# A third seven-product pair in gate and up, and the decay masks of the state-space mixer on ScalarE, in a two-layer hybrid decoder trunk

## The chip, the cores and the metric

The kernel runs on one core of a Trainium2 chip. A core has five engines with an instruction stream each: TensorE (PE, matrix products; its weight loads are listed as PEld), VectorE (DVE), ScalarE (ACT), GpSimd (POOL) and SyncE (SP, which here issues the large DMAs). The metric is the time of one execution on the device in microseconds (us); of several runs the median is given.

## The reference

The input is one sequence of 256 positions and 2048 features in float32. Each of the two layers does:

```
h    = rms_norm(x)
proj = h @ w_in                          # 2048 x 6608 (6672 in the second layer)
y    = concat(retention(proj), mamba2(proj), rwkv7(proj))
x    = x + y @ w_out                     # 2048 x 2048
h    = rms_norm(x)
x    = x + (silu(h @ w_gate) * (h @ w_up)) @ w_down    # d_ff = 5632
```

and a last rms_norm follows. Inside the state-space mixer (mamba2, 16 heads in two groups of 8, chunks of 128 positions) the part that matters here is

```
a        = dt * A                                       # decay logs, per position and head
seg      = a_cum[i] - a_cum[j]
decay_in = exp(where(i >= j, seg, -inf))                # 128 x 128 per head and chunk
y_diag   = ((C B^T) * decay_in) @ x
```

## The kernel before, in words

**Products in three terms.** Every float32 weight tile is split into a high part (`wh`, a cast to the type fp32r that TensorE multiplies) and a low part (`wl`, the difference), the activations likewise (`xh`, `xl`), and a product is the sum of three matmuls: high by high, high by low, low by high.

**The weights' way.** The kernel knows the whole list of its weight tiles in advance (`plan`). `fetch` (L291) issues a DMA of 512 KB per tile on SP's queue into one of 5 buffers `raw`; `split` (L300) makes the halves, with the cast on ScalarE (L307) and the subtraction on VectorE (L308), into 3 buffers each of `wh` and `wl`. `wtile` is called where TensorE's next tile is needed: it splits up to two parts further than that one and keeps fetching ahead of the splits.

**Stages of a layer.** The input projection has 14 groups of columns (`dense`, L366, matmuls L382 to L392), 8 tiles of 256 rows each, taken in the order of a list. While they run, three lanes of generators work through the mixers: `ret` (retention), `ssm` (state space) and one for rwkv. After each half tile `pump` (L162) advances the lanes in turn until one engine's estimated load since then reaches its credit (VectorE 0.35, ScalarE 0.9, POOL 0.8, TensorE 0.8, in us by a simple estimate per instruction). A generator that yields a number waits that many turns. A scheduler then fixes the order of the instructions on each engine; each engine works strictly in that order.

The output projection has 4 groups of 8 tiles; behind each group `post_pair` (L424) transposes the new activations and splits them for the FFN. The FFN runs in a part of 6 and one of 5 blocks of 512 columns; each block is one call of `gate_up` (L1288), 22 in both layers, and each part is followed by its down projection.

**Gate and up.** A call makes four results C: two halves of the rows by gate and up. Its 2048-long sum is cut into 8 pairs `kp` of 128-row tiles. An ordinary pair is eight block products of 128x128 by 128x512, 24 matmuls, in two parts `c` of 12. A pair in the tuple `SEVEN` is treated as a 2x2 block matrix product and takes seven products, by a scheme of the Strassen and Winograd kind, 21 matmuls in three parts: s0 (9), s1 (6) and s2 (6). Four of the seven products collect over the pairs of `SEVEN` in accumulators of their own (`mx` in the profile) and are added into the results once, after the last pair of `SEVEN`, by the additions on VectorE behind L1325. All of these matmuls are recorded as L1294.

For such a pair `split` makes sums of the weight blocks first: `u1` (L329, 1024 wide, from the two tiles of the pair, so both must have landed), the two halves of `u2` (L331, L332, 512 wide each), then three halvings L307/L308 (of the tile itself, of `u1` and of `u2`) and one half-width halving of the fourth block (L335 on ScalarE, L336 on VectorE). An ordinary pair has two halvings. The sums of the activations are made once per layer in `post_pair`: four 128x128 subtractions and additions on POOL (L106), a 512-wide cast on ScalarE and a 512-wide subtraction on VectorE. On the host, `_pairs` lays out the four blocks of such a pair accordingly.

**The masks.** `ssm_dt` (L995) makes the decay logs: for each of four blocks (chunk by group) `masked(i)` multiplies a triangular 128x128 matrix of ones by the decay log of each of 8 heads, for the high part `ah` and the low part `al` of the log. The result, 128x1024 for each part, is multiplied by another triangular matrix on TensorE (L1080, L1081), which sums it to the wanted differences, and ScalarE takes the exponential. The products are one POOL instruction per 128x1024 result (L106, `u<-cc,ah` and `u<-cc,s`), 8 per layer. Also on POOL, and in the same part of the layer, are the inverse square roots of the rwkv lane (L106, with `negh`) and a part of retention's rotary products (L106, `u<-u,cc` 128x256).

Of the kernel before, what the change touches and what calls it, by code (L numbers as in the profile page):

```python
# [9 lines left out]
AF = mybir.ActivationFunctionType  # L10
ALU = mybir.AluOpType
PSUM = bass.MemoryType.PSUM

P = 128
# [9 lines left out]

FFN_PARTS = [6, 5]

SEVEN = (2, 5)

# [27 lines left out]
class Trunk:  # L58
# [194 lines left out]
    def plan(self):  # L253
# [7 lines left out]
        for l in range(DEPTH):  # L261
# [7 lines left out]
            for nf in FFN_PARTS:  # L269
                for f in range(f0, f0 + nf):  # L270
                    for kp in range(8):
                        t = [("wgu", ((l * 11 + f) * 16 + 2 * kp + j) * P * 1024, 512) for j in range(2)]
                        if kp in SEVEN:
                            parts += [(f"s{j}", len(seq)) for j in range(3)]
# [149 lines left out]
    def post_pair(self, kp, src, scale, xh, xl):  # L424
# [10 lines left out]
        self.tt(fl(xl), w[:, :512], fl(xh).bitcast(F32), ALU.subtract)  # L435
        if kp in SEVEN:
            a11, a21, a12, a22, s1, s2, s3, q = [w[:, i * P:(i + 1) * P] for i in range(8)]
# [557 lines left out]
    def ssm_dt(self, l, raw):  # L995
# [17 lines left out]
        p = self.S(33)[:, :32]  # L1013
# [26 lines left out]
        for t in range(2):  # L1040
            o = self.U()
# [9 lines left out]
            self.mm(ps, M["Bt"][:, g * P:(g + 1) * P], xe[:, g * 512:(g + 1) * 512])  # L1051
            self.act(st[:, g * 512:(g + 1) * 512], ps, AF.Copy)
        yield
        tl = self.cst("tril").rearrange("p (o c) -> p o c", o=1).to_broadcast([P, 8, P])

        def masked(i):
            r = []
            for ap in (ah.bitcast(F32), al):
                m = self.U(F32R)
                self.tt(m[:, :1024].rearrange("p (h c) -> p h c", h=8), tl,  # L1060
                        ap[:, 8 * i:8 * i + 8].rearrange("p (h o) -> p h o", o=1).to_broadcast([P, 8, P]),
                        ALU.mult, eng="pool")
                r.append(m)
                yield 2
            return r
        ahead = yield from masked(0)
        y = M["y"] = [None, None]
        dsk = self.par(l, "dsk")
        for t in range(2):
# [3 lines left out]
            for g in range(2):  # L1073
                ma = ahead
                if t + g < 2:
                    ahead = yield from masked(2 * t + g + 1)
# [12 lines left out]
                for j in range(8):  # L1089
                    h = 8 * g + j  # L1090
# [197 lines left out]
    def gate_up(self, rstd):  # L1288
# [9 lines left out]
        for kp in range(8):  # L1298
            xk = [self.xs(2 * kp + j) for j in range(2)]
            A = lambda t, k: tuple(h[:, t * P:(t + 1) * P] for h in xk[k])  # L1300
            if kp not in SEVEN:
                for k in range(2):
# [4 lines left out]
            else:  # L1307
                cb = self.comb[kp]
                S1, S2, S3, Q = [(cb[:, i * P:(i + 1) * P], cb[:, 512 + i * P:512 + (i + 1) * P]) for i in range(4)]
                first, last = kp == SEVEN[0], kp == SEVEN[-1]  # L1310
                if first:
# [11 lines left out]
            if kp == 0:  # L1323
                self.flush()
            if kp == SEVEN[-1]:  # L1325
                t0, t1, sg = self.U(), self.U(), self.U()
# [164 lines left out]
def _pairs(a, b):  # L1491
# [4 lines left out]
    for kp in range(k):  # L1496
        if kp in SEVEN:
            o[kp, 0, :, 0], o[kp, 0, :, 1], o[kp, 1, :, 0], o[kp, 1, :, 1] = \
# [93 lines left out]
```

## Time and profile before

| | |
|---|---|
| median of 3 runs | 2423.09 us (2422.21 to 2423.18) |
| profiled execution | 2423.65 us, of which the span of the instructions is 2421.6 us |
| granted TensorE clock, mean over the span | 0.996 |
| PE busy | 2389.3 us (99% of the span) |
| DVE busy | 1675.4 us (69%) |
| ACT busy | 1206.7 us (50%) |
| POOL busy | 152.1 us (6%) |
| HBM read | 430.66 MB, 179 GB/s over the span |

A row of a timeline gives the start, the duration, the engine, the line, the operation with its output and inputs, and in brackets the engine's idle time before it with the instruction that ended it. A row of the groups gives the count, the busy time and the mean in ns of one instruction, then the idle time before them and its releasers. A row of the windows gives busy time and count for each engine, then the granted clock as a share of the full one, the share of the DMA engines and GB/s. Matmuls are pipelined: their durations overlap, and what one costs is the distance between two starts.

### The profile page before, as it was taken

The page shows a single profiled execution, that of the slowest core. Times are in us where ns is not written, and L with a number is a line of the kernel's source. Part 1 is how long each engine was busy: PE and PEld are TensorE (multiplying, and loading weights), DVE is VectorE, ACT ScalarE, POOL GpSimd, SP SyncE. Part 2 cuts the span into 40 slices and gives each one's busy share as a digit, 9 for nine tenths or more (in the row PEclk, how much of TensorE's full clock was granted, in tenths as well). Part 3 has the DMA queues.
Part 4 walks back from the last instruction along what each step waited for, and adds up shares of the span by engine and source line. Part 5 has one row for each costly group of instructions (what it writes and reads, how often), then busy time and mean ns, then how long its engine had stood idle before and what let it go on. Part 6 is the DMA issues. An engine that isn't in the chain of part 4 may idle for free. (4 is left out here: it accounts for less than half of the span.)

```text
span 2421.6 us, 33651 instructions
## 1 busy us (share of the span) xinstructions
PE 2389.3 (99%) x13076; PEld 2023.5 (84%) x13076; DVE 1675.4 (69%) x2106; ACT 1206.7 (50%) x1506; POOL 152.1 (6%) x157
## 2 busy tenths in 40 slices
PE   8999899999999999999999999999999999999998
PEld 8998788888888878888899988887888888888886
DVE  7777756577886467876558876565878754688754
ACT  6445545555554345554454546455555543455543
POOL 2100320000000000000001113200000000000000
PEclk9999999999999999999999999999999999999999
DMA  8454345556555555565544544445555655555654
GB/s 290 147 170 115 133 154 174 179 184 202 192 197 190 189 188 194 187 213 191 184 164 143 165 122 153 157 165 182 192 195 188 200 191 191 184 197 196 215 187 144
DMA packets 139424, 436.01 MB, mean 180 GB/s; under 512 B 30464, under 2 KB 30720, under 8 KB 139264
## 3 DMA queue, kind: packets, MB, share of 16 engines
q1 hardware_dynamic: 137360, 428.52, 53.4%
q0 software_dynamic: 1184, 4.19, 0.5%
q8 instruction: 102, 1.67, 0.3%
q10 hardware_dynamic: 720, 1.15, 0.1%
q14 instruction: 58, 0.48, 0.1%
HBM read 430.66 MB, written 3.15 MB: 179 GB/s over the span
## 5 line engine op out<-in xcount | busy, mean ns | idle before, releaser
L308 DVE TENSOR_TENSOR wl<-raw,wh 128x1024 fp32r<-128x1024 f32 (+3 forms) x763 | 928.0, 1218 | 494.2 <-ACT wh L307 487.2
L307 ACT ACTIVATE wh<-raw 128x1024 fp32r<-128x1024 f32 (+3 forms) x763 | 793.8, 1042 | 893.1 <-PE dn L391 443.4
L1294 PE MATMUL dn<-wh,xh 128*128 128x512 f32 x1100 | 431.4, 392 | 2.3 <-DVE res L103 2.3
L1294 PE MATMUL dn<-wl,xh 128*128 128x512 f32 x1100 | 428.6, 390 | 0.0
L1294 PE MATMUL dn<-wh,xl 128*128 128x512 f32 x1100 | 428.5, 390 | 0.0
L391 PE MATMUL dn<-wh,u 128*128 128x512 f32 x920 | 363.4, 395 | 0.0
L390 PE MATMUL dn<-wh,u 128*128 128x512 f32 x920 | 363.0, 395 | 0.0
L392 PE MATMUL dn<-wl,u 128*128 128x512 f32 x920 | 362.1, 394 | 0.3 <-DVE wl L308 0.2
L382 PE MATMUL dn<-xh,wh 128*128 128x256 f32 x896 | 258.8, 289 | 7.8 <-ACT wh L307 7.8
L384 PE MATMUL dn<-xh,wl 128*128 128x256 f32 x896 | 254.8, 286 | 1.1 <-DVE wl L308 1.1
L383 PE MATMUL dn<-xl,wh 128*128 128x256 f32 x896 | 255.1, 285 | 0.0
L1294 PEld LDWEIGHTS dn<-wh,xh 128*128 128x128 f32 x1100 | 206.5, 188 | 48.9 <-DVE u L103 3.9
L1294 PEld LDWEIGHTS dn<-wl,xh 128*128 128x128 f32 x1100 | 206.4, 188 | 43.4
L1294 PEld LDWEIGHTS dn<-wh,xl 128*128 128x128 f32 x1100 | 206.6, 188 | 42.1
L390 PEld LDWEIGHTS dn<-wh,u 128*128 128x128 f32 x920 | 172.8, 188 | 40.3 <-DVE u L103 0.8
L392 PEld LDWEIGHTS dn<-wl,u 128*128 128x128 f32 x920 | 172.9, 188 | 39.8 <-DVE wl L308 1.1
L391 PEld LDWEIGHTS dn<-wh,u 128*128 128x128 f32 x920 | 172.8, 188 | 38.7
L382 PEld LDWEIGHTS dn<-xh,wh 128*128 128x128 f32 x896 | 173.7, 194 | 10.5 <-ACT wh L307 8.2
L392 PE MATMUL dn<-wl,xh 128*128 128x512 f32 (+2 forms) x448 | 164.3, 368 | 11.0 <-DVE wl L308 11.0
L384 PEld LDWEIGHTS dn<-xh,wl 128*128 128x128 f32 x896 | 173.1, 194 | 1.8 <-DVE wl L308 1.5
L383 PEld LDWEIGHTS dn<-xl,wh 128*128 128x128 f32 x896 | 173.9, 194 | 0.2
L390 PE MATMUL dn<-wh,xh 128*128 128x512 f32 (+2 forms) x448 | 170.9, 382 | 0.0
(177 smaller groups left out, 2725.6 us busy)
## 6 DMA issues: line engine op xcount, KB each, us to landing
raw<-wgu SPq DMA_DIRECT2D x352, 512.0 KB, 3.8
raw<-wdown SPq DMA_DIRECT2D x176, 512.0 KB, 4.2
raw<-win SPq DMA_DIRECT2D x175, 512.0 KB, 3.5
raw<-wout SPq DMA_DIRECT2D x64, 512.0 KB, 3.3
raw<-win SPq DMA_DIRECT2D x32, 340.0 KB, 2.9
raw<-win SPq DMA_DIRECT2D x16, 360.0 KB, 3.0
u<-xt SPq DMA_DIRECT2D x8, 256.0 KB, 7.2
res<-x SPq DMA_DIRECT2D x4, 512.0 KB, 5.2
```

The costliest lines, as they stand in the source:

```text
L307: nc.scalar.activation(wh[:, c], raw[:, c], AF.Copy)
L308: nc.vector.tensor_tensor(wl[:, c], raw[:, c], wh[:, c].bitcast(F32), op=ALU.subtract)
L382: nc.tensor.matmul(o, lhsT=wh[:, c], rhs=xh, start=st and m % 2 == 0, stop=False)
L383: nc.tensor.matmul(o, lhsT=wh[:, c], rhs=xl, start=False, stop=False)
L384: nc.tensor.matmul(o, lhsT=wl[:, c], rhs=xh, start=False, stop=sp and m % 2 == 1)
L390: nc.tensor.matmul(o, lhsT=xh[:, x], rhs=wh[:, c], start=st, stop=False)
L391: nc.tensor.matmul(o, lhsT=xl[:, x], rhs=wh[:, c], start=False, stop=False)
L392: nc.tensor.matmul(o, lhsT=xh[:, x], rhs=wl[:, c], start=False, stop=sp)
L1294: mm(o, lhsT=x[a], rhs=w[b], start=start and i == 0, stop=stop and i == 2)
```

## The change

The tuple `SEVEN` gets a third member, 4, so that pairs 2, 4 and 5 of the eight take seven products. In `masked`, the one POOL instruction for eight heads becomes eight ScalarE activations (a copy with the head's decay log as a scale per partition), and the generator yields after every four heads where it used to yield 2 after each eight.

```diff
-SEVEN = (2, 5)
+SEVEN = (2, 4, 5)
...
-        tl = self.cst("tril").rearrange("p (o c) -> p o c", o=1).to_broadcast([P, 8, P])
+        tl = self.cst("tril")

         def masked(i):
             r = []
             for ap in (ah.bitcast(F32), al):
                 m = self.U(F32R)
-                self.tt(m[:, :1024].rearrange("p (h c) -> p h c", h=8), tl,
-                        ap[:, 8 * i:8 * i + 8].rearrange("p (h o) -> p h o", o=1).to_broadcast([P, 8, P]),
-                        ALU.mult, eng="pool")
+                for h in range(8):
+                    self.act(m[:, h * P:(h + 1) * P], tl, AF.Copy, scale=ap[:, 8 * i + h:8 * i + h + 1])
+                    if h % 4 == 3:
+                        yield 1
                 r.append(m)
-                yield 2
             return r
```

Over the whole program 66 matmuls, 16 POOL masks and two loads of ScalarE's function table (both in layer 0) go; 128 activations of 128x128 come, and for every call of `gate_up` one each of L329, L331, L332, L336 and L308 on VectorE and of L307 and L335 on ScalarE; per layer, `post_pair` issues four more POOL instructions, one more cast and one more subtraction.

POOL's instructions in layer 0, from the rwkv lane's inverse square roots to the last rotary products, before:

```order
L106 TENSOR_TENSOR s_3164<-s_3164,negh 128x8
L106 TENSOR_TENSOR u_3234<-cc,ah_2981 128x1024
L106 TENSOR_TENSOR u_3269<-cc,s_2983 128x1024
L106 TENSOR_TENSOR u_3310<-cc,ah_2981 128x1024
L106 TENSOR_TENSOR u_3334<-cc,s_2983 128x1024
L106 TENSOR_TENSOR u_3450<-cc,ah_2981 128x1024
L106 TENSOR_TENSOR u_3470<-cc,s_2983 128x1024
L106 TENSOR_TENSOR u_3560<-u_3542,cc 128x4x64 x2
L106 TENSOR_TENSOR u_3620<-cc,ah_2981 128x1024
L106 TENSOR_TENSOR u_3641<-cc,s_2983 128x1024
L106 TENSOR_TENSOR u_3560<-u_3542,cc 128x4x64 x2
L106 TENSOR_TENSOR u_3766<-u_3748,cc 128x4x64 x4
```

Here `negh` marks an inverse square root, `cc,ah` and `cc,s` the masks of the high and low logs, and `128x4x64` the rotary products of q and of k. After the change only the first row and the rotary products are left, in two groups of four. ScalarE's instructions in the same place of the changed kernel, from the first mask on (L307 are the casts of the weights, `dn` and `mx` rows move results out of the accumulators):

```order
L307 ACTIVATE wh_3222<-raw_3070 128x680
L121 ACTIVATE u_3201<-mx_3202 128x512
L121 ACTIVATE u_3234<-cc,ah_2981 128x128 x2
L121 ACTIVATE u_3201<-mx_3205 128x512
L121 ACTIVATE u_3234<-cc,ah_2981 128x128 x2
L307 ACTIVATE wh_3260<-raw_3110 128x680
L121 ACTIVATE u_3234<-cc,ah_2981 128x128 x4
L307 ACTIVATE wh_3283<-raw_3148 128x680
L121 ACTIVATE u_3245<-mx_3246,pp_79 128x256 x2
L121 ACTIVATE u_3245<-mx_3253,pp_79 128x256 x2
L121 ACTIVATE u_3295<-cc,s_2983 128x128 x4
L307 ACTIVATE wh_3307<-raw_3175 128x680
```

The masks stand between the casts, two to eight in a row.

VectorE's instructions around the last pair of `SEVEN` in the second call of `gate_up`, before (L308 with `wl<-raw` halves a tile, with `wl<-u` a sum):

```order
L308 TENSOR_TENSOR wl_5432<-raw_5318,wh_5431 128x1024
L308 TENSOR_TENSOR wl_5450<-raw_5350,wh_5449 128x1024
L329 TENSOR_TENSOR u_5485<-raw_5378,raw_5423 128x1024
L331 TENSOR_TENSOR u_5486<-u_5485,raw_5378 128x512
L308 TENSOR_TENSOR wl_5468<-raw_5376,wh_5467 128x1024
L332 TENSOR_TENSOR u_5486<-u_5486,raw_5423 128x512
L336 TENSOR_TENSOR u_5494<-raw_5423,u_5494 128x512
L308 TENSOR_TENSOR wl_5491<-raw_5378,wh_5490 128x1024
L308 TENSOR_TENSOR wl_5514<-u_5485,wh_5513 128x1024
L308 TENSOR_TENSOR wl_5527<-u_5486,wh_5526 128x1024
```

and in the changed kernel, from the halving of pair 4's own tile to that of pair 5's second sum:

```order
L308 TENSOR_TENSOR wl_5527<-raw_5422,wh_5526 128x1024
L332 TENSOR_TENSOR u_5522<-u_5522,raw_5448 128x512
L336 TENSOR_TENSOR u_5530<-raw_5448,u_5530 128x512
L308 TENSOR_TENSOR wl_5550<-u_5521,wh_5549 128x1024
L329 TENSOR_TENSOR u_5572<-raw_5450,raw_5495 128x1024
L331 TENSOR_TENSOR u_5573<-u_5572,raw_5450 128x512
L308 TENSOR_TENSOR wl_5563<-u_5522,wh_5562 128x1024
L332 TENSOR_TENSOR u_5573<-u_5573,raw_5495 128x512
L308 TENSOR_TENSOR wl_5578<-raw_5450,wh_5577 128x1024
L336 TENSOR_TENSOR u_5581<-raw_5495,u_5581 128x512
L308 TENSOR_TENSOR wl_5595<-u_5572,wh_5594 128x1024
L308 TENSOR_TENSOR wl_5608<-u_5573,wh_5607 128x1024
```

The sums of pair 5 now begin (L329, L331) ahead of the halving of pair 4's second sum (`wl_5563`).

## The prediction

> **What bounds the kernel now.** I read the page's busy table and clock first, then its groups, then the windows of the stages that the change touches, then their timelines.
>
> ```profile
> span 2421.6 us, 33651 instructions
> PE 2389.3 (99%) x13076; PEld 2023.5 (84%) x13076; DVE 1675.4 (69%) x2106; ACT 1206.7 (50%) x1506; POOL 152.1 (6%) x157
> L308 DVE TENSOR_TENSOR wl<-raw,wh 128x1024 fp32r<-128x1024 f32 (+3 forms) x763 | 928.0, 1218 | 494.2 <-ACT wh L307 487.2
> L307 ACT ACTIVATE wh<-raw 128x1024 fp32r<-128x1024 f32 (+3 forms) x763 | 793.8, 1042 | 893.1 <-PE dn L391 443.4
> ```
>
> TensorE is busy for 99% of the span. VectorE waits for ScalarE's casts, and those wait for TensorE (a buffer of wh comes free when TensorE is done with the tile three parts earlier), so TensorE sets the pace and the others follow. A matmul taken out is worth its pitch, unless another engine falls behind. The stages that matter:
>
> ```profile
> core 0: us, PE busy (x) PEld busy (x) DVE busy (x) ACT busy (x) POOL busy (x), PEclk, DMA share, GB/s
> 540.60:584.00 43.40, 43.40 (x196) 35.71 (x195) 34.98 (x39) 22.94 (x25) 0.00 (x0) 1.00 0.58 194
> 258.00:330.00 72.00, 64.78 (x324) 55.85 (x323) 47.69 (x44) 38.97 (x47) 21.87 (x13) 0.95 0.44 150
> 269.30:276.10 6.80, 5.50 (x21) 5.45 (x22) 6.04 (x8) 2.18 (x5) 3.00 (x2) 0.50 0.35 116
> ```
>
> The first row is one period of gate and up (22 in all): TensorE without a gap, VectorE 34.98 of 43.40 (81%). The second is the stretch of layer 0 in which the POOL masks run: TensorE loses 7.2 us, and the third row shows the granted clock at half within it.
>
> **Part 1, products.** Three rows of TensorE's timeline give the price: the second-last block pair of eight products starts at 553.84, the seven-product pair 5 at 559.28, and what follows at 564.15.
>
> ```profile
> 553.84 0.39 PE L1294 MATMUL dn<-wh,xh 128*128 128x512 f32 x1
> 559.28 0.39 PE L1294 MATMUL mx<-wh,xh 128*128 128x512 f32 x1
> 564.15 0.39 PE L1294 MATMUL dn<-wh,xh 128*128 128x512 f32 x1
> ```
>
> Eight products, 24 matmuls, take 5.44 us (0.227 each); seven, 21 matmuls, take 4.87 us (0.232 each, so a little worse than in proportion). The change saves 5.44 − 4.87 = 0.57–0.58 us per call, ×22 = **12.8 us**. Were the new pair to run at the old pitch it would be 3 × 0.227 × 22 = 15.0.
>
> What it adds is VectorE's and ScalarE's, on the weights' way to TensorE. Five rows of VectorE's timeline around pair 5, one of three halvings back to back, and the group of the first sums:
>
> ```profile
> 550.66 1.22 DVE L329 TENSOR_TENSOR u<-raw,raw 128x1024 f32<-128x1024 f32 x1
> 551.92 0.69 DVE L331 TENSOR_TENSOR u<-u,raw 128x512 f32<-128x512 f32 x1
> 553.66 0.68 DVE L332 TENSOR_TENSOR u<-u,raw 128x512 f32<-128x512 f32 x1
> 554.27 0.68 DVE L336 TENSOR_TENSOR u<-raw,u 128x512 fp32r<-128x512 f32 x1
> 557.68 1.23 DVE L308 TENSOR_TENSOR wl<-u,wh 128x1024 fp32r<-128x1024 f32 x1 [1.54 <-ACT wh L307]
> 560.40 1.23 DVE L308 TENSOR_TENSOR wl<-u,wh 128x1024 fp32r<-128x1024 f32 x1 [1.50 <-ACT wh L307]
> 450.42 3.50 DVE L308 TENSOR_TENSOR wl<-raw,wh 128x1024 fp32r<-128x1024 f32 x3 [0.87 <-ACT wh L307]
> L329 DVE TENSOR_TENSOR u<-raw,raw 128x1024 f32<-128x1024 f32 x44 | 53.6, 1219 | 11.8 <-DMA raw<-wgu 11.6
> ```
>
> Start to start, a 1024-wide one costs (3.50 − 1.22)/2 = 1.14 and a 512-wide one 554.27 − 553.66 = 0.61. Per call the change adds L329, L331, L332, L336 and one more L308 (three halvings for two): 1.14 + 3 × 0.61 + 1.14 = 4.1 us. VectorE goes to 39.1 of 42.8 us (91%): it still fits. It doesn't fit locally. Pairs 4 and 5 are now neighbours, and each asks 4 × 1.14 + 3 × 0.61 = 6.4 us of VectorE against 4.87 us of TensorE: 12.8 against 9.7, a deficit of 3.0 us. Its cover is the look-ahead: splits stand two parts ahead of TensorE, 5.4 us in parts of the eight-product kind, and VectorE idles some 1.5 us per part wherever a part needs one halving only (rows 557.68 and 560.40). Carrying the rows along the new order, the tightest tiles (the second sums' wl of pair 4, the first wl of pair 5) come 0.9 to 1.2 us before TensorE needs them. The new order also puts pair 5's L329, which needs a DMA to have landed, in front of pair 4's last wl; that wait was 11.6 us over 44 instructions and cost TensorE nothing, and I charge a late one now and then. I take 0.05 us per call, **1 us** in all; the ends are 0 and, without look-ahead, 3.0 per call (a rival below). ScalarE's added 1.6 us on 22.94 of 43.40 is covered. DMA moves the same bytes in the same order.
>
> The x side gets one more combination per layer, in the output projection: four POOL 128x128, one 512 cast, one 512 subtract.
>
> ```profile
> 443.77 2.54 POOL L106 TENSOR_TENSOR u<-u 128x128 f32<-128x128 f32 x4 [49.75 <-ACT u L121]
> L308 DVE TENSOR_TENSOR wl<-raw,wh 128x1024 fp32r<-128x1024 f32 x14 | 16.9, 1224 | 11.3 <-ACT wh L307 11.3
> ```
>
> The second row is the wl group from 440 to 480, where two such combinations run: 1224 ns as everywhere, with 11.3 us of VectorE idle ahead of it. I take **0**, since the products need the combination only in the FFN's fifth pair.
>
> The Trainium skill, "SBUF — State Buffer", section "SBUF: two separate sides", speaks against these POOL instructions: of VectorE and GpSimd, whichever starts first keeps the shared port pair for a whole instruction, where both read SBUF. By it eight added ones of about 0.7 us would block VectorE for up to 5.8 us; the wl group shows no such lengthening beside the combinations, though the masks below do.
>
> **Part 2, masks off POOL.** The first six rows are of layer 0's timeline, the other three of layer 1's:
>
> ```profile
> 260.52 1.89 POOL L106 TENSOR_TENSOR u<-cc,ah 128x1024 fp32r<-128x1024 f32 x1
> 260.58 7.44 DVE L113 TENSOR_SCALAR u<-u,s,s 128x64 f32<-128x64 f32 x4 [1.75 <-POOL s L106]
> 269.78 2.52 POOL L106 TENSOR_TENSOR u<-cc,s 128x1024 fp32r<-128x1024 f32 x1
> 264.26 0.31 PE L391 MATMUL dn<-wh,xl 128*128 128x340 f32 x1
> 267.94 2.60 DVE L308 TENSOR_TENSOR wl<-raw,wh 128x680 fp32r<-128x680 f32 x1
> 270.60 0.65 PE L392 MATMUL dn<-wl,xh 128*128 128x340 f32 x1 [6.02 <-DVE wl L308]
> 1482.21 0.40 PE L391 MATMUL dn<-wh,xl 128*128 128x512 f32 x1
> 1484.96 0.97 DVE L113 TENSOR_SCALAR u<-u,s,s 128x64 f32<-128x64 f32 x4
> 1485.09 0.50 PE L392 MATMUL dn<-wl,xh 128*128 128x512 f32 x1 [2.48 <-DVE wl L308]
> ```
>
> Six masks run back to back on POOL, 1.89 us for the first five and 2.52 for the last, begun at 269.78. Beside them four small TENSOR_SCALARs of VectorE take 7.44 us, one per mask; without a mask beside them the same four take 0.97 (row 1484.96). A subtract behind them takes 2.60. So wl is late, and TensorE stands from 264.26 to 270.60: 6.34 less one pitch of about 0.16, **6.2 us**. Behind it the clock is 0.50 until 276.1 (the third window above): of the 5.5 us that TensorE works in it, half, **2.7**, are lost. Layer 1 has the same thing shorter: 1485.09 − 1482.21 − 0.227 = **2.65**, without a clock dip. With the masks gone from POOL nothing of this remains.
>
> A second wait comes from masks that stand on POOL between the two halves of the rotary products of q:
>
> ```profile
> 316.09 1.89 POOL L106 TENSOR_TENSOR u<-cc,s 128x1024 fp32r<-128x1024 f32 x1
> 319.41 1.22 DVE L103 TENSOR_TENSOR u<-u,u 128x1024 f32<-128x1024 f32 x1 [5.04 <-POOL u L106]
> 320.84 0.39 PE L391 MATMUL dn<-wh,xl 128*128 128x512 f32 x1
> 322.43 0.50 PE L392 MATMUL dn<-wl,xh 128*128 128x512 f32 x1 [1.20 <-DVE wl L308]
> 1522.65 0.50 PE L392 MATMUL dn<-wl,xh 128*128 128x512 f32 x1 [1.28 <-DVE wl L308]
> ```
>
> VectorE waits 5.04 us for POOL, with a wl queued behind, and TensorE loses 322.43 − 320.84 − 0.227 = 1.36 us; in layer 1 about the same, 2.8 in both. Without masks POOL is done some 4.2 us sooner, but in the new order the waiting add stands one wl earlier. I credit **1.8** of the 2.8.
>
> **Part 3, masks on ScalarE.** 128 activations of 128x128 with a per-partition scale aren't in the trace. The nearest rows, three of the groups and one of ScalarE's timeline:
>
> ```profile
> L121 ACT ACTIVATE s<-dn,s 128x16 f32<-128x16 f32 x4 | 1.1, 275 | 0.8 <-PE dn L392 0.8
> L121 ACT ACTIVATE u<-u,pp 128x256 f32<-128x256 f32 x56 | 26.0, 500 | 7.5 <-DVE u L117 4.4 <-DVE u L103 2.8
> L121 ACT ACT_TABLE_LOAD x18 | 23.1, 1283 | 3.6 <-DVE s L103 2.1 <-PEq L1587 1.2
> 291.28 2.00 ACT L307 ACTIVATE wh<-raw 128x1024 fp32r<-128x1024 f32 x2
> ```
>
> Between 16 and 256 columns, 128 gives 0.38 us; two 1.06 us casts end 2.00 us after the first began, so one overlaps the next by about 0.1, and the pitch is near **0.29**. The bounds are 0.2 and 0.50. In layer 0 that is 64 × 0.29 = 18.6 us on top of 38.97, less two table loads of 1.28 that the new order drops: 55 us in a stretch that shrinks from 72 to some 62. It is 89% full, and a cast behind eight masks comes 2.3 us late, against casts that stand 2 tiles of 2.7 us ahead. Carried along the order, casts just arrive, a few with no slack: I charge **1 us** for both layers. At 0.50 each ScalarE would need 32 us per layer for them, 68 in all, and be some 6 us short in each layer, 13 in both.
>
> **Sum.** −12.8 − 6.2 − 2.7 − 2.65 − 1.8 + 1 + 1 = −24.1 us. The profiled execution took 2423.65 (span 2421.6 and 2.05 around it), 0.56 above the median of 2423.09: 2399.5 on its scale, **2399 us** on that of the median.
>
> **Rivals.** (a) *VectorE becomes the bound at pairs 4 and 5.* Against it stand the idle 1.5 us per part ahead of the pairs and 91% over the call. For it: 12.8 against 9.7 us at that place, in-order waits for DMA at L329. Without any cover it costs 3.0 − 0.58 net, and the call would be slower by 2.4: 22 × 3.0 = 66 us back, 2465. It is slower than before once the wait passes 1.1 us per call (24 of gain and 1 charged, over 22).
> (b) *The masks' stall moves to ScalarE.* Its casts come late in the same stretches: from over 1 up to 13 us, so 2400 to 2411; a gap of 6 us may bring the half clock with it, as above. For it: 89% full; against it: masks come in fours with casts between.
> (c) *A part of the products' gain is given back*, 0.3 to 0.5 us per call, by VectorE or by a weight landing late: 2405 to 2410. The skill's rule on the port pair would add at most 5.8 us by the rows above, 2405, were VectorE's idle time no cover; I give it 0.03 of (c).
> (d) *The change doesn't do what it says for POOL*: VectorE's slow instructions have another cause and the stall stays. Then only the products come: 2399 + 11 + 2 = 2412. Against it: one instruction per mask, in both layers.
>
> **How the numbers follow.** Forecast (2391 to 2404) 0.60, (b) 0.12, (c) 0.13, (d) 0.03, (a) 0.12, of which 0.08 slower than before, 0.03 around no change and 0.01 still faster. The low end is the products at 15.0, all of the rotary wait and nothing charged: 2399 − 2.2 − 1 − 2, some 2 more for clock and pinches that I haven't seen: 2391. The high end takes in (b), (c) and (d): 2412. Measured differences under 0.2% (4.8 us) can't be told from none: faster 0.89, same 0.03, slower 0.08.
>
> **What would show it.** Right: matmuls of gate and up fall by 66; a call lasts 42.8 us; VectorE about 39 in it; no L392 wait of 2.5 us or more near 260 to 275 and 1480 to 1485; clock 1.00 there; masks on ScalarE near 0.38 us long. Wrong: gaps before matmuls of L1294 with releaser DVE wl or u; L307 late behind L121 128x128; L329 waiting for DMA with TensorE idle behind it. The forecast falls if a call lasts over 43.4 us.

## The result and the profile after

The changed kernel takes 2403.93 us (median of 4 runs, 2400.83 to 2405.99) against 2422.65 us of the kernel before in the same job: a ratio of 0.9925, with a 95% interval of 0.9907 to 0.9942. Two later jobs gave 2399.94 (ratio 0.9911, 0.9898 to 0.9925) and 2399.31 (0.9905, 0.9889 to 0.9922). By the medians of these three jobs the change is worth 18.7, 21.1 and 21.4 us. The profiled execution took 2400.83 us, the fastest of the four, and its span is 22.6 us shorter than that of the profile before.

The page of the changed kernel, its first two lines:

```profile
span 2399.0 us, 33852 instructions
PE 2375.1 (99%) x13010; PEld 2006.9 (84%) x13010; DVE 1741.3 (73%) x2218; ACT 1270.7 (53%) x1678; POOL 120.2 (5%) x149
```

TensorE has 66 matmuls fewer and still works for 99% of the span; VectorE is busy for 66 us more than before and ScalarE for 64 more.

**Gate and up.** The timeline of TensorE in the second call, where pair 4, pair 5 and the next pair begin, and a window of 43 us there (us, then busy time and count for PE, PEld, DVE, ACT and POOL, the granted clock, the DMA share and GB/s):

```profile
547.72 0.39 PE L1294 MATMUL mx<-wh,xh 128*128 128x512 f32 x1
552.59 0.39 PE L1294 MATMUL mx<-wh,xh 128*128 128x512 f32 x1
557.45 0.39 PE L1294 MATMUL dn<-wh,xh 128*128 128x512 f32 x1
531.00:574.00 43.00, 43.00 (x195) 35.29 (x194) 38.79 (x44) 24.54 (x28) 0.00 (x0) 1.00 0.60 197
```

Both neighbours take 4.87 us, as one seven-product pair did before, and TensorE has no gap although VectorE is busy for 38.79 of 43.00. From the first to the last matmul of a call, the 22 calls together go from 954.5 to 941.4 us: 13.1 us less. Most calls take 42.7 us; the first takes 44.1, and there the timelines of VectorE and TensorE show a wait that the new order on VectorE brings:

```profile
496.06 1.23 DVE L329 TENSOR_TENSOR u<-raw,raw 128x1024 f32<-128x1024 f32 x1 [3.10 <-DMA raw<-wgu]
497.20 1.22 DVE L308 TENSOR_TENSOR wl<-u,wh 128x1024 fp32r<-128x1024 f32 x1
498.47 0.50 PE L1294 MATMUL mx<-wl,u 128*128 128x512 f32 x1 [1.08 <-DVE wl L308]
```

The first sum of pair 4 waits 3.10 us for a weight tile to land; the halving behind it, which pair 2 still needs, is late by that, and TensorE stands for 1.08 us.

**The masks in layer 0.** The timeline where the stall was, and the group of the new masks:

```profile
260.26 0.98 DVE L113 TENSOR_SCALAR u<-u,s,s 128x64 f32<-128x64 f32 x4 [1.75 <-POOL s L106]
261.15 0.86 DVE L308 TENSOR_TENSOR wl<-raw,wh 128x680 fp32r<-128x680 f32 x1
265.00 1.27 ACT L121 ACTIVATE u<-cc,ah 128x128 fp32r<-128x128 f32 x4
L121 ACT ACTIVATE u<-cc,ah 128x128 fp32r<-128x128 f32 x64 | 20.4, 395 | 0.0
258.00:321.00 63.00, 61.77 (x323) 53.16 (x322) 36.56 (x43) 49.65 (x101) 5.44 (x5) 1.00 0.55 178
```

The four small TENSOR_SCALARs take 0.98 us where they took 7.44. TensorE's gap of 6.02 us is gone, and the granted clock is 1.00 over the stretch. The masks take 395 ns each and four of them 1.27 us, a pitch of 0.29. ScalarE is busy for 49.65 of 63 us (79%), and no gap of TensorE names it there.

**The rotary wait stays.** Timelines of VectorE and TensorE in layer 0, TensorE's in layer 1, and two rows of a new gap in layer 0:

```profile
306.47 1.23 DVE L103 TENSOR_TENSOR u<-u,u 128x1024 f32<-128x1024 f32 x1 [2.03 <-POOL u L106]
308.89 0.50 PE L392 MATMUL dn<-wl,xh 128*128 128x512 f32 x1 [1.15 <-DVE wl L308]
1500.95 0.50 PE L392 MATMUL dn<-wl,xh 128*128 128x512 f32 x1 [0.57 <-DVE wl L308]
389.90 0.48 DVE L117 SCALAR_TENSOR_TENSOR u<-mx,pp,u 128x256 fp32r<-128x256 f32 x1 [1.88 <-ACT u L121]
391.86 1.06 PE L133 MATMUL mx<-cc,u 128*128 128x128 f32 x8 [0.68 <-DVE u L103]
```

VectorE waits 2.03 us for POOL instead of 5.04, but the add stands a tile earlier, and TensorE's gap in layer 0 is 1.15 as against 1.20; in layer 1 it fell from 1.28 to 0.57. The last row is a new gap of 0.68. The state-space lane now ends inside the output projection: its last subtraction on VectorE (389.90) waits 1.88 us for ScalarE, the last product of the retention lane stands behind it on VectorE, and the transposes of that product on TensorE (391.86) wait.

### The profile page after: what moved, and what is told of

Read it like the earlier page. It is cut to its first block, busy times and chain, and to the rows that moved or that the text cites. A ratio compares the mean times of both kernels' runs of the same rounds, so it can differ in the third digit from the quotient of the medians.

```text
span 2399.0 us, 33852 instructions
## 1 busy us (share of the span) xinstructions
PE 2375.1 (99%) x13010; PEld 2006.9 (84%) x13010; DVE 1741.3 (73%) x2218; ACT 1270.7 (53%) x1678; POOL 120.2 (5%) x149
## 3 DMA queue, kind: packets, MB, share of 16 engines
q10 hardware_dynamic: 720, 1.15, 0.1%
## 4 chain that ended last, share of the span: by engine, by line
PE 94%; DVE 2%; ACT 2%; DMA 1%; issue 1%; POOL 0%; SPq 0%; DVEq 0%; ACTq 0%; POOLq 0%
PE dn L1294 30%; PE dn L392 12%; PE dn L390 12%; PE dn L391 12%; PE mx L1294 8%; PE dn L382 4%; PE dn L384 4%; PE dn L383 4%; PE mx L129 4%; PE mx L133 2%; ACT u L121 1%; DVE wl L308 1%; PE mx L537 1%; DMA raw<-wgu 1%; ACT wh L307 1%
## 5 line engine op out<-in xcount | busy, mean ns | idle before, releaser
L308 DVE TENSOR_TENSOR wl<-raw,wh 128x1024 fp32r<-128x1024 f32 (+3 forms) x741 | 895.4, 1212 | 469.4 <-ACT wh L307 462.9
L307 ACT ACTIVATE wh<-raw 128x1024 fp32r<-128x1024 f32 (+3 forms) x741 | 768.9, 1040 | 800.1 <-PE dn L391 416.6
L1294 PE MATMUL dn<-wh,xh 128*128 128x512 f32 x946 | 371.6, 393 | 1.6 <-DVE res L103 1.6
L1294 PE MATMUL dn<-wh,xl 128*128 128x512 f32 x946 | 368.7, 390 | 0.0
L1294 PE MATMUL dn<-wl,xh 128*128 128x512 f32 x946 | 368.6, 390 | 0.0
L392 PE MATMUL dn<-wl,u 128*128 128x512 f32 x920 | 362.6, 394 | 0.3
L307 ACT ACTIVATE wh<-u 128x1024 fp32r<-128x1024 f32 x132 | 140.3, 1063 | 153.4 <-PE dn L1294 60.1
L1294 PEld LDWEIGHTS dn<-wh,xh 128*128 128x128 f32 x946 | 177.6, 188 | 42.2 <-DVE u L103 3.9
L1294 PEld LDWEIGHTS dn<-wl,xh 128*128 128x128 f32 x946 | 177.6, 188 | 37.3
L392 PEld LDWEIGHTS dn<-wl,u 128*128 128x128 f32 x920 | 173.2, 188 | 41.5 <-DVE wl L308 2.0
L1294 PEld LDWEIGHTS dn<-wh,xl 128*128 128x128 f32 x946 | 177.7, 188 | 36.0
L382 PEld LDWEIGHTS dn<-xh,wh 128*128 128x128 f32 x896 | 173.2, 193 | 10.4 <-ACT wh L307 8.1
```

Source lines behind the costliest of these rows:

```text
L307: nc.scalar.activation(wh[:, c], raw[:, c], AF.Copy)
L308: nc.vector.tensor_tensor(wl[:, c], raw[:, c], wh[:, c].bitcast(F32), op=ALU.subtract)
L382: nc.tensor.matmul(o, lhsT=wh[:, c], rhs=xh, start=st and m % 2 == 0, stop=False)
L392: nc.tensor.matmul(o, lhsT=xh[:, x], rhs=wl[:, c], start=False, stop=sp)
L1294: mm(o, lhsT=x[a], rhs=w[b], start=start and i == 0, stop=stop and i == 2)
```

## The experiments

Times of this section are medians; the kernel before took 2421.03, 2421.94 and 2420.74 us in the three jobs of the experiments. Differences in us are those of the medians. Single runs scatter by 2 to 3 us around the median (the kernel before from 2418.4 to 2425.2), so differences of 2 us between kernels are read from the profiles.

**The changed kernel again, and each half alone.** The first job of the experiments; the first run has no edit:

> The changed kernel once more, with more rounds, since its four runs lie at 2400.8, 2402.0, 2405.9 and 2406.0 and its profile is of the first. My theory (products 14 us, the masks' stalls 11 us, 0.8 us of the rotary wait, a loss of 1.2 in the first call of gate and up) gives 2400 to 2402 and wants a further loss of some 4 us in the other runs, at a place of the mixers where casts have no slack. The rival, that the gain itself is smaller than the profile says, gives no such place and a steady 2404.

It took 2399.94 us (2399.07 to 2400.27). No further loss of 4 us appears. A smaller difference that I can point to is at the start of the program, in the window of the first 30 us, of the first profile and of this one:

```profile
0.00:30.00 30.00, 21.25 (x141) 20.43 (x142) 19.72 (x27) 20.04 (x31) 11.81 (x13) 0.95 0.88 331
```

```profile
0.00:30.00 30.00, 20.82 (x153) 19.99 (x154) 19.82 (x27) 21.00 (x33) 11.92 (x13) 1.00 0.88 333
```

While the first weights arrive, the granted clock was 0.95 in one execution and 1.00 in the other, and 12 fewer matmuls were through by the end of the window. The kernel before had 0.95 there too. Whether the clock made the difference isn't shown: the fastest version below had 0.94 there, with 151 matmuls. The first matmul of gate and up came 1.2 us later in the first profile than in this one (481.5 and 480.3), and waits for DMA of about 1 us come and go between executions. The two runs at 2406 had mean granted clocks of 0.995 and 0.997, against 0.998 and 0.999 of the two faster ones; where in them the clock was lower isn't known, since neither was profiled.

```diff
-SEVEN = (2, 5)
+SEVEN = (2, 4, 5)
```

> Three seven-product pairs, masks still on POOL. Theory: 22 calls shorter by 0.63 us each as in the profile of the changed kernel, less 1.2 in the first call: 13 us faster than before, 2409 to 2411; the stalls of 6.2 and 2.65 us and the half clock in the input projection stay. Rival (the products' gain is given back by VectorE): 2414 to 2420.

It took 2412.70 us, a ratio of 0.9963 (0.9950 to 0.9977): 8.3 us faster, less than the 13 expected and outside the range, though the interval reaches to 12. In its profile the calls of gate and up sum to 941.7 us as in the changed kernel, 12.8 less than before, and the span is 11.5 shorter (2410.1). Why the medians differ by less isn't shown; the one profile of the kernel before is of an execution of 2423.65 us, above the 2421.03 of this job. The stalls of the masks are there unchanged, by TensorE's and VectorE's timelines:

```profile
260.15 7.44 DVE L113 TENSOR_SCALAR u<-u,s,s 128x64 f32<-128x64 f32 x4 [1.75 <-POOL s L106]
270.18 0.65 PE L392 MATMUL dn<-wl,xh 128*128 128x340 f32 x1 [6.03 <-DVE wl L308]
```

The masks alone, with `SEVEN = (2, 5)`:

> Masks on ScalarE, two seven-product pairs as before. Theory: the stalls of 6.2 and 2.65 us and the half clock go, 0.8 of the rotary wait goes: 11 us faster, 2409 to 2413, and it adds up with the run of the products alone to the whole change. Rival (the stall moves to ScalarE's casts): 2415 to 2420.

It took 2410.67 us, 0.9956 (0.9943 to 0.9968): 10.4 us faster, as expected. The two halves give 8.3 + 10.4 = 18.7 us, and the whole change 21.1 in the same job: they add up within their intervals. The first matmul of gate and up marks the end of the input and output projections of layer 0. Its start stands behind the durations in these rows, of the products alone and of the changed kernel's first profile, which both had a clock of 0.95 in the first 30 us:

```profile
L1294 PE MATMUL dn<-wh,xh x946: 387/389/499, 488.8 to 2287.9; 128*128 128x512 f32 x190
```

```profile
L1294 PE MATMUL dn<-wh,xh x946: 387/389/501, 481.5 to 2276.6; 128*128 128x512 f32 x190
```

488.8 against 481.5: the masks are worth 7.3 us before the FFN of layer 0. The kernel before stood at 488.3 (same clock), the masks alone at 480.2 (clock 1.00 at the start, as in the changed kernel's second profile with 480.3).

**Is it the length of one POOL instruction?** Two seven-product pairs, masks on POOL, but one instruction per head (the lines that stand in place of ScalarE's activations):

```diff
+                for h in range(8):
+                    self.tt(m[:, h * P:(h + 1) * P], tl, ap[:, 8 * i + h:8 * i + h + 1].to_broadcast([P, P]), ALU.mult, eng="pool")
+                yield 2
```

> Two seven-product pairs as before, masks still on POOL, but head by head: 128 POOL instructions of 128x128 for 16 of 128x1024. Theory (a VectorE instruction that meets a POOL instruction waits for the whole of that one instruction): with short ones the four TENSOR_SCALARs take 0.4 to 0.7 us each instead of 1.88, the gap of 6.2 us near 264 shrinks below 2, the half clock behind it goes, 5 to 10 us faster than before, 2411 to 2417. Rival (POOL's total time counts, not the length of one instruction): POOL is busy for longer, 64 x 0.6 us per layer against 8 x 1.9, and the gaps stay or grow: 2421 to 2435.

It took 2414.41 us, 0.9967 (0.9956 to 0.9978): 7.5 us faster than before, with POOL doing the same products. VectorE's and POOL's timelines in the same place, and the window of layer 0 that the prediction shows:

```profile
260.10 1.46 DVE L113 TENSOR_SCALAR u<-u,s,s 128x64 f32<-128x64 f32 x4 [1.75 <-POOL s L106]
260.04 3.53 POOL L106 TENSOR_TENSOR u<-cc,ah 128x128 fp32r<-128x128 f32 x8
261.48 1.11 DVE L308 TENSOR_TENSOR wl<-raw,wh 128x680 fp32r<-128x680 f32 x1
261.83 1.02 POOL L106 TENSOR_TENSOR u<-cc,ah 128x128 fp32r<-128x128 f32 x1
258.00:330.00 72.00, 70.39 (x366) 60.28 (x364) 46.36 (x48) 43.53 (x54) 46.72 (x70) 1.00 0.53 172
```

The four TENSOR_SCALARs take 1.46 us against 7.44: each now waits for a POOL instruction of 0.39 instead of one of 1.89. The gap of 6 us and the half clock are gone, although POOL is busy for 46.72 us of the window instead of 21.87. So the stall came from the length of a single POOL instruction and the order in which the two engines' instructions alternated, and POOL's total time didn't matter. "Rival (POOL's total time counts)" falls. That agrees with the Trainium skill, "SBUF — State Buffer", section "SBUF: two separate sides", by which a GpSimd instruction and a VectorE instruction in a 2-port mode, or one with two SBUF inputs beside a GpSimd instruction that reads SBUF, exclude each other on a shared port pair, and the one that starts first keeps it to its end. Whether these TENSOR_SCALARs ran in such a mode, no trace here shows. The rotary wait grew here, to gaps of 1.61 and 1.69 us in the two layers, since the masks still stand in POOL's queue.

**Does ScalarE hide the masks?** In the changed kernel, the first block's masks are used for all four blocks, so 96 of 128 activations are left out and the state-space mixer's result is another:

```diff
         def masked(i):
+            if i:
+                yield 4
+                return first
...
-        ahead = yield from masked(0)
+        ahead = first = yield from masked(0)
```

> The changed kernel with the masks of the first of the four blocks used for all four, so 96 of the 128 activations are left out (the result of the state-space mixer is then another). Theory (ScalarE hides the masks): at most 1.5 us faster than the changed kernel. Rival (casts come late behind the masks): 3 to 9 us faster.

It took 2401.17 us, 0.9918 (0.9903 to 0.9932), no faster than the changed kernel's 2399.3 to 2399.9. The same window of layer 0:

```profile
258.00:321.00 63.00, 62.83 (x325) 53.61 (x324) 37.58 (x41) 42.48 (x63) 5.81 (x5) 1.00 0.55 181
```

ScalarE has 7 us less to do, TensorE works 1.1 us more of the window, about what the rotary wait cost, which this run doesn't have. The median shows no gain from leaving out 96 activations. It can't exclude a cost of 1 to 2 us, since this run lacks the rotary wait in both layers and has a new gap of 0.66 us in layer 1. The changed kernel's profile has no gap of TensorE over 0.15 us behind the first 30 us that a late cast ended.

**Neighbouring pairs.** Pairs 1, 3 and 5 in the changed kernel, and pairs 3, 4 and 5, with the same number of every instruction:

```diff
-SEVEN = (2, 4, 5)
+SEVEN = (1, 3, 5)
```

> The changed kernel with pairs 1, 3 and 5 in place of 2, 4 and 5, so that no two seven-product pairs are neighbours; the same number of every instruction. Theory (the look-ahead covers the neighbours): calls as long as with 2, 4, 5 (42.7 us), total within 1.5 us of the changed kernel. Rival (neighbours pinch VectorE): 2 to 4 us faster than the changed kernel.

```diff
-SEVEN = (2, 4, 5)
+SEVEN = (3, 4, 5)
```

> The changed kernel with pairs 3, 4 and 5, three neighbours, the same number of every instruction. VectorE needs 6.4 us for each pair against 4.87 of TensorE, a deficit of 4.6 us over three; over two it was 3.0, hidden with some 1 us to spare. Theory (the look-ahead is a stock of about 4 us that neighbours use up): TensorE waits 0.3 to 1 us per call at the third pair, calls of 43.0 to 43.7 us, 2406 to 2420 in all. Rival (only the mean load of a call counts): calls of 42.7 and 2399 to 2402.

Pairs 1, 3, 5 took 2397.45 us (0.9900, 0.9887 to 0.9914), 2.5 less than the changed kernel in that job. That is more than the 1.5 of my theory and inside the rival's 2 to 4, though the intervals overlap. The profiles speak for the theory: most calls take 42.6 to 42.9 us, about as there, and only the wait in the first call is smaller. Pairs 3, 4, 5 took 2400.24 (0.9911, 0.9896 to 0.9926) beside 2399.31 of the changed kernel: three neighbours cost nothing clear either, with calls of 42.7 to 43.1 us. My theory of a stock that neighbours use up falls, and the timeline of VectorE and TensorE shows what it left out:

```profile
541.55 1.22 DVE L329 TENSOR_TENSOR u<-raw,raw 128x1024 f32<-128x1024 f32 x1
550.12 0.39 PE L1294 MATMUL mx<-wh,xh 128*128 128x512 f32 x1
531.00:574.00 43.00, 43.00 (x194) 35.33 (x193) 38.73 (x45) 24.42 (x27) 0.00 (x0) 1.00 0.58 198
```

The first sum of pair 5 begins at 541.55, 8.6 us before TensorE begins that pair (550.12). The three buffers of wh and wl limit the halvings to two parts ahead, but the sums lie in buffers of another kind and run further ahead, as far as the weights have landed. That this lead covers the neighbours is argued from these rows; no run shortens it. Over a call VectorE's load is 38.73 of 43.00 us, which fits, as with the pairs apart.

**Four pairs.** That load can be pushed over TensorE's:

```diff
-SEVEN = (2, 4, 5)
+SEVEN = (1, 3, 5, 6)
```

> The changed kernel with four seven-product pairs, 1, 3, 5 and 6. VectorE was busy 34.98 us of a call with two and 38.79 with three, so four ask 42.6, against 42.07 of TensorE by 42.72 less 0.65. Theory (VectorE becomes the bound here): calls of 42.5 to 43.2 us, no gain over three pairs, 2396 to 2408 in all. Rival (TensorE still sets the pace): calls of 42.1, 2384 to 2387.

It took 2397.71 us (0.9903, 0.9888 to 0.9918), no more gain than with three. The window of the second call and TensorE's waits (us in total, times, longest):

```profile
531.00:574.00 43.00, 42.93 (x193) 34.83 (x191) 42.20 (x49) 25.82 (x30) 0.00 (x0) 1.00 0.60 197
PE dn L1294 <- DVE u L336: 5.5, 16, 0.8
```

VectorE is busy for 42.20 of 43.00 us, most calls take 42.8 to 42.9 us, no less than with three pairs, and TensorE now waits 16 times for a sum. The list counts only whole gaps. In a typical call the two matmuls at that sum start 0.7 and 0.55 us after the one before, instead of 0.23, and so lose 0.8 us, more than the 0.65 that the fourth pair was to bring. So rival (a) of the prediction, VectorE as the bound, is real one pair further on. It ends in a draw and not in a loss: with VectorE as the bound a call is about as long as VectorE's work.

**The rotary wait.** In the changed kernel, the rotary products on VectorE:

```diff
-            self.tt(bv[:, :, 0:64], xv[:, t, :, 64:128], tb("nsin").to_broadcast([P, 4, 64]), ALU.mult, eng="pool")
-            self.tt(bv[:, :, 64:128], xv[:, t, :, 0:64], tb("sin").to_broadcast([P, 4, 64]), ALU.mult, eng="pool")
+            self.tt(bv[:, :, 0:64], xv[:, t, :, 64:128], tb("nsin").to_broadcast([P, 4, 64]), ALU.mult)
+            self.tt(bv[:, :, 64:128], xv[:, t, :, 0:64], tb("sin").to_broadcast([P, 4, 64]), ALU.mult)
```

> The changed kernel with the rotary products of q and k on VectorE instead of POOL. Theory (the remaining wait of the add for POOL costs TensorE 1.3 us in layer 0 and 0.74 in layer 1): these two gaps go, about 2 us faster than the changed kernel, 2397 to 2399. Rival (VectorE's added 16 instructions of 0.36 us make its next wl as late as POOL did): no change.

It took 2398.06 us (0.9904, 0.9888 to 0.9921). Both gaps are gone: of TensorE's waits (us in total, times, longest) those before L392 are 1.7 us in two places in the changed kernel's second profile, the first row below; in this kernel, the second row, it is one of 0.2, which lies in the output projection of layer 1. The 1.3 to 1.9 us between the medians are within the scatter.

```profile
PE dn L392 <- DVE wl L308: 1.7, 2, 1.1
PE dn L392 <- DVE wl L308: 0.2, 1, 0.2
```

**A version that is faster than both.** Pairs 1, 3 and 5 and the rotary products on VectorE, beside the changed kernel in one job:

> Pairs 1, 3 and 5 and the rotary products on VectorE, the two runs that were fastest taken together. Theory: 2 us below the changed kernel from the rotary wait and up to 2 from the first call, 2395 to 2398. Rival (both were within the scatter of runs): 2398 to 2400.

> The changed kernel beside the two above, for a comparison in the same job: 2399 to 2404.

2394.69 us (2392.96 to 2396.79; 0.9889, 0.9874 to 0.9904) against 2399.31 (2397.68 to 2400.42). That is 4.6 us less, just under the expected range, and 26.0 below the kernel before. No run of the one overlaps the other's, so this version is faster. How the 4.6 us divide between the rotary wait (2.05 us by the gaps), the first call and scatter wasn't measured.

## Why the prediction was right, point by point

The forecast was 2399 us, 24 faster; measured were 18.7 in the job of the result, 21.1 and 21.4 in the two later ones. The mechanisms came as forecast. The 2403.93 us of the result lie at the very end of the range of 2391 to 2404, while the two later medians lie within 1 us of 2399; the sum below comes so close to the forecast because errors in its terms cancel.

- **Products**, −12.8 and 1 us charged for VectorE. Measured 13.1 less over the 22 calls, the charge included. The pair's length was predicted to 0.01 us: in a typical call pair 4 goes from 5.44 to 4.86. The call's 42.8 was 42.7; the further 0.06 a call lies in pair 2 (4.86 to 4.80), appears with the masks alone too, so it isn't a gain of the products, and its cause is open. VectorE's 39.1 us per call was 38.8. The charge came true as one event, and not where I put it: pair 4's first sum waited for a late DMA in front of pair 2's last halving, where I had named pair 5's in front of pair 4's. It cost 1.24 us in the first profile and less in the second.
- **The deficit at pairs 4 and 5** was rightly taken as covered, but probably by the wrong stock. I counted two parts of look-ahead; the sums run further ahead than the halvings, and three neighbours, where my count gave a wait, cost nothing clear. The break-even of 1.1 us per call was never near.
- **The masks' stall**, −6.2 − 2.7 in layer 0 and −2.65 in layer 1. Both gaps and the half clock are gone, in the changed kernel and with the masks alone, and the run with short POOL instructions shows the mechanism.
- **The rotary wait**, −1.8. This term was mis-sized: the two gaps fell from 2.8 us of lost time to 2.05, so 0.75. I had seen that the add moves a wl earlier and took too little for it.
- **ScalarE**, +1. The pitch of 0.29 came out. Leaving 96 masks out gained nothing, so the term is 0 within the scatter. ScalarE was busy for 79% of the window shown, which holds 58 of the layer's 64 masks, and not for 89%.
- **The activations' sums**, 0. The products alone reach gate and up 0.5 us later in layer 0 (488.8 against 488.3), and take 0.3 less for the projections of layer 1 (474.0 against 474.3), so this holds.
- **Not in the sum**: the state-space lane ends later, VectorE's work for the retention lane is held up behind it, and the output projection of layer 0 has a gap of 0.68 us.

By the starts of matmuls, the first profiles of before and after, one execution each, differ by 6.8 us up to the FFN of layer 0 (488.3 to 481.5; the prediction's terms there sum to 9.3, with half of the rotary and ScalarE's terms), by 3.9 in the input and output projections of layer 1 (474.3 to 470.4, or 472.0 in the second profile; terms: 3.05) and by 13.1 in the calls (term: 11.8). So layer 0 gave 2.5 less than forecast: 0.85 is the rotary wait that stayed, 0.84 the lost time at the new gap, and some 0.8 I can't put to a place. The three differences are 23.8 of the forecast's 24 because what layer 0 fell short by came in elsewhere, 1.3 of it in the calls; that is luck. The spans differ by 22.6, since about 1 us is lost elsewhere, and the medians by less still. By the profiles the rivals (b), (c) and (d) didn't come; (a) needs a fourth pair.

## What to carry to other kernels

On an engine that sets the pace, a saved instruction is worth its pitch as long as every feeding engine's work per round stays below the new round; that sum predicted both the gain of the third pair and the end of the gain at the fourth. What buffers limit the look-ahead has to be asked for each kind of instruction, not once for the engine. Where VectorE and POOL work at the same time, long POOL instructions beside short VectorE ones were the costly combination here (four TENSOR_SCALARs of 7.44 us against 1.46): shorter POOL instructions, or another engine, took the stall away.

## What the runs showed of the hardware that I had not expected

A small VectorE instruction that meets a row of POOL instructions goes through one for one with them: four of 64 columns took 7.44 us beside masks of 1.89 us, 1.46 beside masks of 0.39, and 0.98 alone. And it is mutual: the POOL instruction beside the wl of 1.11 us took 1.02 us, where the others of its row took 0.39. Beside the small TENSOR_SCALARs POOL kept its pace.
